# A decoder block's first products: the first round of four k tiles taken as two rounds of two, with the first weights split earlier

## The chip, the cores and the metric

The kernel runs on one core of a Trainium2 chip. The metric is the time of one execution on the device in microseconds (us); of several runs the median counts. The core has four computing engines with an instruction queue each, worked in order: TensorE (PE; PEld in the profile is its loading of weights), VectorE (DVE), ScalarE (ACT) and GpSimd (POOL). A fifth queue, SP, issues the loads from device memory.

## The reference

One decoder layer on 256 tokens of width 2048, in float32. Its first step is a norm whose scale and shift come from a second input vector c by a large product, and the normed tokens h then meet the input weights w_in (2048 x 19008):

```python
mod = (c_act @ w_mod[l] + b_mod[l])[:, None, :]
sh1, sc1, g1, sh2, sc2, g2 = jnp.split(mod, 6, axis=-1)
h = rmsnorm(x, norm1_w[l]) * (1.0 + sc1) + sh1
x = x + g1 * mixer(h, rel_bias, w_in[l], ...)       # attention and state space branch
h = rmsnorm(x, norm2_w[l]) * (1.0 + sc2) + sh2
x = x + g2 * swiglu(h, w_ffn_in[l], w_ffn_out[l])
...
proj = h @ w_in
q, k, v, z, xbc, dt_raw, g_attn, g_ssm = jnp.split(proj, ...)
```

A product with one row, as c_act @ w_mod, reads 2048 x 2048 weights for each of sh1 and sc1 and has almost no arithmetic. Everything behind the first norm waits for it.

## The kernel before

**Weights.** All weights of the large products come as one stream of chunks of 512 rows (four k tiles of 128) by 512 columns, 1 MB each, loaded by SP into a ring of three buffers (`load_chunk`, L321). A float32 weight is split in two parts for TensorE: `hi` by a cast on ScalarE (L338) and `lo = w - hi` on VectorE (L340), two k tiles (128 x 1024 numbers) at a time. `products` makes three products of each k tile and each piece of 128 columns: hi with the tokens' high part (L373), hi with their low part (L375), lo with their high part (L376). For q, k, B and C ("cm1") a chunk is 48 products of 128x256; for v ("tm", L394 to L396) it is 24 of 128x512. `Stream.run` takes a chunk from the queue, emits the split of the next one, then the chunk's products. So the instructions of each engine stand in the order in which this Python code emits them; nothing reorders them later.

**The first rounds.** The eleven groups of 512 columns that are needed first (three of q, k and v each, one of B and C each) are not run over all sixteen k tiles at once. `ROUNDS` cuts the k tiles in four rounds of four. For a round only the matching 512 columns of sh1 and sc1 must be known. While the products of one round run, VectorE works out shift and scale for the next: for each of 16 k tiles and both sections one multiply-add of 128x512 (L623 for the first, L625 for the others) into `sums`, whose 128 partitions TensorE adds up at the end (`reduce_to`, L600). Then three small VectorE instructions finish scale and shift (L632, L633, L635), and `split_affine` applies them to the turned tokens and splits the result in high (ScalarE, L312) and low (VectorE, L314 and L315) parts. In the loop the multiply-adds of two k tiles are followed by as many chunks as are due (`while st.queue ...`), and `TAILCH = 2` chunks are kept back so that TensorE has work while the next shift and scale are finished.

**Sums of the rounds.** The first group (q of the first heads) keeps its sums in two PSUM banks through all rounds. The other ten groups leave PSUM at the end of each round: the first time by a copy on ScalarE (L488), later by an addition on VectorE (L490, 128x512 from PSUM), two per chunk.

**The very start.** Before the first round there is nothing for TensorE but the turning of the tokens (16 transposes for the first four pairs of k tiles, L463, and 16 more in the middle). In the first round two of the sixteen k tiles of w_mod, `ONPE = (11, 15)`, are summed by TensorE itself, without VectorE. The first chunk is split after the tokens' affine. `BIASR` names the loop pass in which the attention biases are built (L580 on TensorE); the small vectors are prepared in the first pass.

**Behind the rounds** the same stream goes on to the end of the kernel, and the rest of w_mod is summed by VectorE in a task that only fills room.

Of the kernel before, what the change touches and what calls it, by code (L numbers as in the profile page):

```python
# [16 lines left out]
P = 128  # L17
# [16 lines left out]
def bucket_onehot():  # L34
    """[33, 3, 384]: column i stands for the query-key distance 255 - i of a group's
    dilation; row b is one where the distance is attended and falls in bucket b, row 32
    where it is not attended."""
# [20 lines left out]
class Stream:  # L58
    """The weights as one stream of 512-row chunks.  Each chunk is split in its float32r parts
    one chunk ahead of its products; the other work is cut in steps (generators that yield the  # L60
    kind of their next step: "D" with its VectorE and ScalarE time, "P" with the PSUM banks it
    takes, or "W" to wait until it is asked for) that are laid between the chunks, as far as the
    engines have room beside the splits.  Tasks of rank LAST only fill what the others leave."""
# [25 lines left out]
    def _force(self, t):  # L89
        """the next step of t, once the banks it needs are free"""  # L90
# [41 lines left out]
    def run(self, budget, until=0):  # L132
        """emits the chunks of the queue but for the last `until`, which the next call sees first"""
# [19 lines left out]
def tile_hybrid_block(  # L153
# [88 lines left out]
    # kept where base + channel_multiplier * p + pattern . column compares true with 0  # L242
# [21 lines left out]
    def mod_load(sec, c0, n, kc):  # L264
        """the k tiles of 512 rows and n columns of w_mod"""
# [15 lines left out]
    def rstd_of(ss, n, w):  # L281
        """1/sqrt(ss/n + eps) of the sums ss [P, w]"""
# [6 lines left out]
    def pool_rstd(ss, n):  # L289
        """1/sqrt(ss/n + eps) of ss [P, 2] on GpSimd: Newton's steps from  # L290
        the usual first guess, whose exponent comes from the integer view"""
# [14 lines left out]
    def act_of(tiles):  # L306
        """kt -> the [P, 512] (high | low) parts of that k tile"""
        return lambda kt: tiles[kt // 2][:, kt % 2, :]

    def split_affine(dst, src, s, b):  # L310
        """dst (high | low) of src * s + b"""
# [13 lines left out]
    def split_chunk(ch):  # L325
        raw = load_chunk(ch)
        got = []
        if ch["kind"] == "dt":
            # (high | low) side by side
# [14 lines left out]
    def products(ch):  # L344
# [34 lines left out]
        else:  # L379
            # "first": the second half of the tokens waits for the group's last chunk  # L380
# [211 lines left out]
    for r, (k0, nk) in enumerate(ROUNDS):  # L592
# [16 lines left out]
        for kc in range(4):  # L609
            ws = [mod_load(sec, k0 * P, nt, kc) for sec in range(2)]  # L610
            for k in range(4):
                kk = kc * 4 + k
                if r == 0 and kk in ONPE:
                    for sec in range(2):
                        reduce_to(sec, ws[sec][k], cs[:, kk:kk + 1])
                    if kk == ONPE[0]:
                        for kp in range(NEARLY, KT // 2):
                            turn_x(kp)
# [784 lines left out]
```

## Time and profile before

| | before |
|---|---|
| median of 3 runs | 2054.4 us (2054.11 to 2054.72) |
| span of the profiled execution | 2053.7 us |
| TensorE busy | 2010.1 us (98%) |
| VectorE busy | 1454.7 us (71%) |
| ScalarE busy | 999.4 us (49%) |
| bytes moved | 469.17 MB, mean 228 GB/s |
| granted TensorE clock, mean | 0.992 of full speed |

The span is the profiled execution from its first to its last instruction; it lies 0.7 us under the median of the runs. Busy time is the time with an instruction of the engine under way. Of instructions that overlap, as TensorE's and VectorE's do by a little, a group's mean is longer than the spacing from one to the next; where spacing matters it is taken from two starts. A granted clock of 1.00 is 2.4 GHz, 0.50 is 1.2 GHz.

### The profile page before, as it was taken

What the parts mean: (1) busy time and instruction counts of PE and PEld (TensorE: products, weight loads), DVE (VectorE), ACT (ScalarE), POOL (GpSimd) and SP (SyncE); (2) the same over time, 40 slices, a digit from 0 to 9 for tenths busy, and PEclk for the clock granted to TensorE, in tenths of its full rate; (3) what the DMA queues carried; (4) which work ended last, traced back from release to release, by engine and by line L of the source; (5) the groups of instructions that cost most, each with busy time, mean ns of one, the idle gap of its engine ahead of it and who ended that gap; (6) DMA issues with size and microseconds to landing.
All of it is one profiled execution on the core that took longest, in us unless ns stands there. A gap on an engine that the chain in (4) does not pass through costs nothing.

```text
span 2053.7 us, 31324 instructions
## 1 busy us (share of the span) xinstructions
PE 2010.1 (98%) x12720; PEld 1801.2 (88%) x12720; DVE 1454.7 (71%) x1941; ACT 999.4 (49%) x1391; POOL 95.0 (5%) x176
## 2 busy tenths in 40 slices
PE   4999999999999999999999999999999999999998
PEld 3999999999999999888888888788888888888886
DVE  5788987876777776886877787876755555555564
ACT  4444335465566565554544444644444344444443
POOL 1000000000111110110000000100000000000000
PEclk7999999999999999999999999999999999999999
DMA  9898684575656565677767777587865555555553
GB/s 342 294 346 286 226 268 154 170 251 173 223 189 223 200 216 175 216 268 264 267 230 279 270 265 286 185 287 245 287 205 177 195 202 185 195 195 185 188 195 129
DMA packets 218337, 469.17 MB, mean 228 GB/s; under 512 B 10403, under 2 KB 10591, under 8 KB 218192
## 3 DMA queue, kind: packets, MB, share of 16 engines
q1 hardware_dynamic: 214080, 453.61, 64.3%
q0 software_dynamic: 4112, 13.56, 2.1%
q8 instruction: 99, 1.62, 0.3%
q14 instruction: 46, 0.38, 0.1%
HBM read 464.95 MB, written 2.18 MB: 227 GB/s over the span
## 4 chain that ended last, share of the span: by engine, by line
PE 94%; DVE 2%; DMA 1%; ACT 1%; issue 1%; POOL 1%; SPq 0%; ACTq 0%; DVEq 0%; POOLq 0%
PE pa L359 28%; PE pa L361 14%; PE pa L373 9%; PE pa L376 9%; PE pa L375 9%; PE pa L394 6%; PE pa L395 6%; PE pa L396 6%; DMA s<-in_w_mod_dram 1%; PE pb L960 1%; DVE lo L340 1%; PE pb L600 1%; PE pb L674 1%; DVE ma L625 1%; PE pb L978 0%
## 5 line engine op out<-in xcount | busy, mean ns | idle before, releaser
L340 DVE TENSOR_TENSOR lo<-w,hi 128x1024 fp32r<-128x1024 f32 x664 | 791.0, 1229 | 453.8 <-ACT hi L338 448.6
L338 ACT CAST hi<-w 128x1024 fp32r<-128x1024 f32 x664 | 668.2, 1048 | 646.6 <-PE pa L359 251.3
L359 PE MATMUL pa<-s,hi 128*128 128x512 f32 x2496 | 881.9, 399 | 1.6 <-DVE s L1271 1.4
L361 PE MATMUL pa<-s,lo 128*128 128x256 f32 x2496 | 697.9, 280 | 0.0
L359 PEld LDWEIGHTS pa<-s,hi 128*128 128x128 f32 x2496 | 468.7, 188 | 118.0 <-DVE s L1271 2.5
L373 PE MATMUL pa<-s,hi 128*128 128x256 f32 x1664 | 478.4, 288 | 3.6 <-ACT hi L338 3.6
L376 PE MATMUL pa<-s,lo 128*128 128x256 f32 x1664 | 472.1, 284 | 1.4 <-DVE lo L340 1.4
L361 PEld LDWEIGHTS pa<-s,lo 128*128 128x128 f32 x2496 | 470.5, 189 | 1.7 <-issue 1.2
L375 PE MATMUL pa<-s,hi 128*128 128x256 f32 x1664 | 472.0, 284 | 0.0
L373 PEld LDWEIGHTS pa<-s,hi 128*128 128x128 f32 x1664 | 320.4, 193 | 7.4 <-ACT hi L338 4.4
L376 PEld LDWEIGHTS pa<-s,lo 128*128 128x128 f32 x1664 | 320.4, 193 | 1.7 <-DVE lo L340 1.7
L375 PEld LDWEIGHTS pa<-s,hi 128*128 128x128 f32 x1664 | 320.6, 193 | 1.1 <-issue 1.0
L394 PE MATMUL pa<-hi,s 128*128 128x512 f32 x576 | 225.9, 392 | 0.0
L395 PE MATMUL pa<-lo,s 128*128 128x512 f32 x576 | 224.3, 389 | 0.7 <-DVE lo L340 0.7
L396 PE MATMUL pa<-hi,s 128*128 128x512 f32 x576 | 224.2, 389 | 0.0
L668 DVE SCALAR_TENSOR_TENSOR ma<-wm,cs,ma 128x512 f32<-128x512 f32 x240 | 164.4, 747 | 0.0
L395 PEld LDWEIGHTS pa<-lo,s 128*128 128x128 f32 x576 | 108.1, 188 | 24.1 <-DVE lo L340 1.5
L394 PEld LDWEIGHTS pa<-hi,s 128*128 128x128 f32 x576 | 108.1, 188 | 23.7 <-ACT s L488 0.6
L396 PEld LDWEIGHTS pa<-hi,s 128*128 128x128 f32 x576 | 108.1, 188 | 22.7
L436 ACT COPY t<-pa 128x256 f32<-128x256 f32 x120 | 44.6, 373 | 98.0 <-PE pa L361 92.5
L625 DVE SCALAR_TENSOR_TENSOR ma<-s,cs,ma 128x512 f32<-128x512 f32 x116 | 79.2, 746 | 1.8 <-DMA s<-in_w_mod_dram 1.7
L834 DVE SCALAR_TENSOR_TENSOR s<-s,v,s 128x255 f32<-128x255 f32 (+1 forms) x144 | 64.7, 519 | 0.0
(238 smaller groups left out, 1083.0 us busy)
## 6 DMA issues: line engine op xcount, KB each, us to landing
w<-in_w_in_dram SPq DMA_DIRECT2D x148, 1024.0 KB, 5.2
w<-in_w_ffn_in_dram SPq DMA_DIRECT2D x88, 1024.0 KB, 5.0
wm<-in_w_mod_dram SPq DMA_DIRECT2D x64, 1024.0 KB, 5.1
w<-in_w_ffn_out_dram SPq DMA_DIRECT2D x44, 1024.0 KB, 5.1
s<-in_w_mod_dram SPq DMA_DIRECT2D x64, 512.0 KB, 9.5
w<-in_w_ssm_proj_dram SPq DMA_DIRECT2D x32, 1024.0 KB, 5.2
w<-in_w_out_dram SPq DMA_DIRECT2D x16, 1024.0 KB, 5.1
s<-acd POOLq DMA_DIRECT2D x16, 512.0 KB, 4.7
```

The source lines that it names most:

```text
L338: A_.copy(hi, raw[:, k:k + 2, :])
L340: V.tensor_tensor(lo, raw[:, k:k + 2, :], hi, op=OP.subtract)
L359: PE.matmul(accs[n], hi[:, n * P:(n + 1) * P], a, start=(kk == first), stop=False, skip_group_check=True)
L361: PE.matmul(accs[n][:, :S], lo[:, n * P:(n + 1) * P], a[:, :S], start=False, stop=(kk == last), skip_group_check=True)
L373: PE.matmul(o, w1, a[:, :S], start=(kk == first and n % 2 == 0), stop=False, skip_group_check=True)
L375: PE.matmul(o, w1, a[:, S:], start=False, stop=False, skip_group_check=True)
L376: PE.matmul(o, w2, a[:, :S], start=False, stop=(kk == last), skip_group_check=True)
L394: PE.matmul(o, xh, hi, start=(kk == first), stop=False)
L395: PE.matmul(o, xh, lo, start=False, stop=False)
L396: PE.matmul(o, xl, hi, start=False, stop=(kk == last))
L625: V.scalar_tensor_tensor(d, ws[sec][k], cs[:, kk:kk + 1], d, op0=OP.mult, op1=OP.add)
L668: V.scalar_tensor_tensor(a[:, i, :], w[:, 2 * k + i, :], cs[:, kk:kk + 1], a[:, i, :], op0=OP.mult, op1=OP.add)
```

## The change

The first round is cut in two rounds of two k tiles. For these two, w_mod is loaded in 256 columns (a load is again 512 KB, but of four k tiles with rows of 1 KB), the multiply-adds are 128x256, and the chunks of w_in are of two k tiles and 512 KB. In the first round TensorE sums three k tiles of w_mod, 7, 13 and 15, instead of 11 and 15; the second half of the turning moves with the first of them, from 11 to 7, and five matmuls of 128x512 whose result is not used follow it. The first round's chunks are queued ahead of the tokens' affine, and the first two of them are split there; before it was one, and behind the affine. `BIASR` goes from 2 to 3, which is the same pair of k tiles as before. The change also drops comments and docstrings, which are left out here.

```diff
-    # pairs of k tiles of x turned at once; k tiles of w_mod that TensorE sums in the first round
-    NEARLY, ONPE = 4, (11, 15)
+    NEARLY, ONPE = 4, (7, 13, 15)
...
-    ROUNDS = [(0, 4), (4, 4), (8, 4), (12, 4)]
+    ROUNDS = [(0, 2), (2, 2), (4, 4), (8, 4), (12, 4)]
...
-    TAILCH, BIASR = 2, 2
+    TAILCH, BIASR = 2, 3
...
                     if kk == ONPE[0]:
                         for kp in range(NEARLY, KT // 2):
                             turn_x(kp)
+                    if kk == 7:
+
+                        ps = misc()
+                        for i in range(5):
+                            PE.matmul(ps, ones, flat(xt[0][0])[:, :512], start=True, stop=True)
                     continue
...
         V.tensor_tensor(sh1[:, k0:k0 + nk], cols[:, :nk], bmT[:, k0:k0 + nk], op=OP.add)
+        if r == 0:
+
+            first_chunks(k0, nk)
+            for ch in st.queue[:2]:
+                ch["parts"] = st.split(ch)
         for kt in range(k0, k0 + nk):
             split_affine(hx[kt // 2][:, kt % 2, :], xnT[kt // 4][:, kt % 4, :],
                          sc1[:, kt:kt + 1], sh1[:, kt:kt + 1])
-        first_chunks(k0, nk)
-        if r == 0:
-            st.queue[0]["parts"] = st.split(st.queue[0])
+        if r:
+            first_chunks(k0, nk)
         st.run(PHASE0, len(first))
```

**Where instructions stand on TensorE ahead of the first products.** Each row is a line, the operation, the tile that is written and those that are read, and the size; `s_` are loaded pieces of w_mod or of x, `cs` the activated c, `pa` the first group's sums. Before, from the last transposes of the second half on:

```order
L463 MATMUL pb_278<-ident,s_97 128x128
L463 MATMUL pb_278<-ident,s_101 128x128
L600 MATMUL pb_205<-cs,s_286 128x1 x4
L600 MATMUL pb_205<-cs,s_290 128x1 x4
L600 MATMUL pb_205<-ones,ma_204 128x1 x8
L373 MATMUL pa_179<-s_171,hi_335 128x256
```

And in the changed kernel:

```order
L463 MATMUL pb_250<-ident,s_97 128x128
L463 MATMUL pb_250<-ident,s_101 128x128
L623 MATMUL pb_256<-s_96,ones 128x512
L623 MATMUL pb_256<-s_96,ones 128x512 x4
L600 MATMUL pb_205<-cs,s_274 128x1
L600 MATMUL pb_205<-cs,s_274 128x1
L600 MATMUL pb_205<-cs,s_276 128x1
L600 MATMUL pb_205<-cs,s_276 128x1
L600 MATMUL pb_205<-cs,s_274 128x1 x2
L600 MATMUL pb_205<-cs,s_276 128x1 x2
```

The five idle matmuls (L623) stand ahead of the last two k tiles of w_mod and of the sums, and each k tile now takes four matmuls where it took eight.

**VectorE between shift and scale and the first products.** Before, the affine of four k tiles (`s_126` turned tokens, `s_171` and `s_172` their parts) comes ahead of the first chunk's lo:

```order
L635 TENSOR_TENSOR sh_120<-pb_205,v_109 128x4
L314 TENSOR_SCALAR t_318<-s_126,sc_121,sh_120 128x256
L315 TENSOR_TENSOR s_171<-t_318,s_171 128x256
L314 TENSOR_SCALAR t_322<-s_126,sc_121,sh_120 128x256
L315 TENSOR_TENSOR s_171<-t_322,s_171 128x256
L314 TENSOR_SCALAR t_326<-s_126,sc_121,sh_120 128x256
L315 TENSOR_TENSOR s_172<-t_326,s_172 128x256
L314 TENSOR_SCALAR t_330<-s_126,sc_121,sh_120 128x256
L315 TENSOR_TENSOR s_172<-t_330,s_172 128x256
L340 TENSOR_TENSOR lo_337<-w_333,hi_335 128x1024
L340 TENSOR_TENSOR lo_341<-w_333,hi_339 128x1024
```

In the changed kernel:

```order
L640 TENSOR_TENSOR sh_120<-pb_205,v_109 128x2
L340 TENSOR_TENSOR lo_301<-w_297,hi_299 128x1024
L340 TENSOR_TENSOR lo_307<-w_303,hi_305 128x1024
L314 TENSOR_SCALAR t_310<-s_126,sc_121,sh_120 128x256
L315 TENSOR_TENSOR s_171<-t_310,s_171 128x256
L314 TENSOR_SCALAR t_314<-s_126,sc_121,sh_120 128x256
L315 TENSOR_TENSOR s_171<-t_314,s_171 128x256
```

The two lo (now of two chunks) have moved ahead of the affine, and half of the affine is left.

**VectorE in the middle of a round.** `ma` are the running sums of w_mod, `pa` a group's products in PSUM. Before, in the third round, from one chunk's lo to the next:

```order
L340 TENSOR_TENSOR lo_1961<-w_1957,hi_1959 128x1024
L340 TENSOR_TENSOR lo_1965<-w_1957,hi_1963 128x1024
L490 TENSOR_TENSOR s_534<-pa_1967,s_534 128x512
L490 TENSOR_TENSOR s_534<-pa_1968,s_534 128x512
L625 SCALAR_TENSOR_TENSOR ma_1804<-s_1947,cs,ma_1804 128x512
L625 SCALAR_TENSOR_TENSOR ma_1804<-s_1951,cs,ma_1804 128x512
L625 SCALAR_TENSOR_TENSOR ma_1804<-s_1947,cs,ma_1804 128x512
L625 SCALAR_TENSOR_TENSOR ma_1804<-s_1951,cs,ma_1804 128x512
L340 TENSOR_TENSOR lo_2027<-w_2023,hi_2025 128x1024
```

In the changed kernel, in the second round of two k tiles:

```order
L340 TENSOR_TENSOR lo_847<-w_843,hi_845 128x1024
L490 TENSOR_TENSOR s_422<-pa_849,s_422 128x512
L490 TENSOR_TENSOR s_422<-pa_850,s_422 128x512
L630 SCALAR_TENSOR_TENSOR ma_749<-s_833,cs,ma_749 128x512
L630 SCALAR_TENSOR_TENSOR ma_749<-s_837,cs,ma_749 128x512
L630 SCALAR_TENSOR_TENSOR ma_749<-s_833,cs,ma_749 128x512
L630 SCALAR_TENSOR_TENSOR ma_749<-s_837,cs,ma_749 128x512
L340 TENSOR_TENSOR lo_885<-w_881,hi_883 128x1024
```

A chunk has one lo here instead of two; the additions and the multiply-adds beside it are as many and as wide as before.

## Rows read from the trace of the kernel before

**Rows 1.** Page: TensorE's busy share, and the chain that ended last, by engine.

```profile
PE 2010.1 (98%) x12720; PEld 1801.2 (88%) x12720; DVE 1454.7 (71%) x1941; ACT 999.4 (49%) x1391; POOL 95.0 (5%) x176
PE 94%; DVE 2%; DMA 1%; ACT 1%; issue 1%; POOL 1%; SPq 0%; ACTq 0%; DVEq 0%; POOLq 0%
```

**Rows 2.** Busy us (x instructions) by round: PE, PEld, DVE, ACT, POOL; clock, DMA, GB/s.

```profile
107.19:174.85 67.66, 67.66 (x481) 62.86 (x481) 59.38 (x83) 28.13 (x34) 0.00 (x0) 1.00 0.85 302
174.85:242.02 67.17, 66.51 (x477) 61.98 (x477) 61.38 (x85) 25.12 (x28) 0.00 (x0) 1.00 0.81 283
```

**Rows 3.** Waits of TensorE between 46 and 250 us: total, times, longest.

```profile
PE pa L373 <- ACT hi L338: 3.6, 1, 3.6
PE pa L376 <- DVE lo L340: 1.4, 1, 1.4
PE pa L395 <- DVE lo L340: 0.7, 2, 0.4
```

**Rows 4.** Timeline to the first products: start, us, engine, instructions [idle before].

```profile
18.10 0.49 DVE L623 TENSOR_SCALAR ma<-s,cs 128x512 f32<-128x512 f32 x1 [0.88 <-DMA s<-in_w_mod_dram]
...
19.89 3.46 PE L463 MATMUL pb<-ident,s 128*128 128x128 f32 x15 [1.60 <-ACT s L457]
...
22.53 0.59 ACT L465 COPY s<-pb 128x512 f32<-128x512 f32 x1 [0.27 <-PE pb L463]
...
32.06 3.74 PE L463 MATMUL pb<-ident,s 128*128 128x128 f32 x16
...
34.43 3.40 DVE L625 SCALAR_TENSOR_TENSOR ma<-s,cs,ma 128x512 f32<-128x512 f32 x5 [1.36 <-DMA s<-in_w_mod_dram]
...
38.87 3.55 PE L600 MATMUL pb<-ones,ma 128*128 128x1 f32 x16
42.46 0.16 DVE L632 TENSOR_TENSOR sc<-pb,v 128x4 f32<-128x4 f32 x1 [4.62 <-PE pb L600]
...
48.21 0.58 PE L376 MATMUL pa<-s,lo 128*128 128x256 f32 x1 [1.36 <-DVE lo L340]
```

**Rows 5.** Busy us, clock, DMA share and GB/s in stretches of the start.

```profile
24.00:27.00 3.00, 0.00 (x0) 0.00 (x0) 3.00 (x6) 0.00 (x0) 0.00 (x0) 1.00 1.05 388
...
28.00:54.00 26.00, 20.21 (x93) 19.38 (x93) 18.92 (x33) 8.20 (x12) 0.00 (x0) 0.50 1.05 386
```

```profile
48.21:54.31 6.10, 6.10 (x28) 6.10 (x29) 6.10 (x9) 0.63 (x1) 0.00 (x0) 0.50 1.05 384
```

**Rows 6.** Timeline of VectorE in the third round, one step.

```profile
206.41 2.73 DVE L625 SCALAR_TENSOR_TENSOR ma<-s,cs,ma 128x512 f32<-128x512 f32 x4
209.05 2.36 DVE L340 TENSOR_TENSOR lo<-w,hi 128x1024 fp32r<-128x1024 f32 x2
211.32 1.28 DVE L490 TENSOR_TENSOR s<-pa,s 128x512 f32<-128x512 f32 x2
212.52 2.73 DVE L625 SCALAR_TENSOR_TENSOR ma<-s,cs,ma 128x512 f32<-128x512 f32 x4
```

**Rows 7.** VectorE's groups by shape, whole span: busy us, mean ns.

```profile
L668 DVE SCALAR_TENSOR_TENSOR ma<-wm,cs,ma 128x512 f32<-128x512 f32 x240 | 164.4, 747 | 0.0
...
L834 DVE SCALAR_TENSOR_TENSOR s<-s,v,s 128x255 f32<-128x255 f32 x48 | 20.9, 477 | 0.0
```

**Rows 8.** Timeline of VectorE: first of four affine pairs, and what follows the fourth.

```profile
107.66 0.41 DVE L314 TENSOR_SCALAR t<-s,sc,sh 128x256 f32<-128x256 f32 x1
...
111.20 2.36 DVE L340 TENSOR_TENSOR lo<-w,hi 128x1024 fp32r<-128x1024 f32 x2
```

**Rows 9.** As group 2: five chunks of 48 products, then three of v.

```profile
193.33:222.52 29.19, 29.19 (x242) 28.95 (x241) 27.42 (x37) 10.01 (x11) 0.00 (x0) 1.00 0.92 329
222.52:240.15 17.63, 16.97 (x75) 13.41 (x74) 17.43 (x22) 5.57 (x6) 0.00 (x0) 1.00 0.55 177
```

**Rows 10.** Timeline of TensorE at full clock: one 128x512 float32 matmul; one set of sums.

```profile
130.13 1.02 PE L580 MATMUL pb<-s,flip 128*128 128x512 f32 x2
```

```profile
105.21 1.95 PE L600 MATMUL pb<-ones,ma 128*128 128x1 f32 x16
107.02 0.36 PE L373 MATMUL pa<-s,hi 128*128 128x256 f32 x1
```

**Rows 11.** DMA issues, whole span: the load with rows of 256 bytes (us to landing).

```profile
w<-in_w_in_dram SPq DMA_DIRECT2D x1, 512.0 KB, 4.1
```

## The prediction

> **What bounds the kernel now.** I read the page first: TensorE is busy 98% of the span and holds 94% of the chain that ended last [rows 1]. So the time is the moment at which TensorE begins its products, plus their sum, plus every pause between them; another engine counts only where it makes such a pause. The waits of TensorE come next: after the start there are almost none, 0.7 us in all between 48 and 250 us [rows 3]. The busy times by round [rows 2], cut where the three small VectorE instructions follow the sums of w_mod (107.19, 174.85, 242.02 us), show the two engines running side by side: in 67.66 and 67.17 us TensorE fills 67.66 and 66.51, VectorE 59.38 and 61.38. VectorE nearly is a second bound there. In a full round its steady step is four multiply-adds (2.64 us), two lo splits (2.27) and two additions from PSUM (1.20), together 6.11 us [rows 6], while TensorE needs 29.19 / 5 = 5.84 us for a chunk of q, k, B or C, and (17.63 - 0.7) / 3 = 5.64 for one of v [rows 3, 9]. The reader should see that VectorE's step is already the longer one; TensorE lives there on work that VectorE had done ahead.
>
> The start is the other stretch [rows 4]. A 512 KB load of w_mod lands every (34.43 - 18.10) / 12 = 1.36 us, the sixteenth at 35.7; TensorE then has two k tiles and the sums left, its last sum begins after 42 us, VectorE gets shift and scale at 42.46, and the products run without a pause from 48.21. TensorE's clock is at half (1.2 GHz) for them until 54.31: 28 products in 6.10 us [rows 5], against 28 x 0.122 = 3.4 at full speed [rows 9], so 2.7 us are lost.
>
> **The start after the change.** Eight loads come ahead of the first products where sixteen did. At the same rate the eighth lands at 18.10 + 5 x 1.36 = 24.9. Its rows are of 1 KB, and no row shows such a load. From below I take 1.36 us each; from above the load in rows of 256 bytes, which took 4.1 us to land [rows 11]: if a load costs a share for its bytes and one for its rows, (4.1 - 1.36) / 1792 = 1.5 ns is the most a row can cost, so 1.75 us a load, and the eighth lands by 28.0. VectorE has 26 instructions of 256 columns ahead of the sums. The multiply-add takes 477 ns at 255 columns and 747 at 512 [rows 7], so its spacing of 0.66 becomes 0.39, and 26 of them from 16.7 end near 27 or 29. Neither is what the sums wait for, because TensorE's own queue is later: sixteen transposes end at 23.35 [rows 4]; k tile 7 (8 recorded instructions, between the full-speed 0.11 of [rows 10] and the half-speed 3.55 / 16 = 0.22 of [rows 4]) ends at 24.4; sixteen more transposes, paced by four copies of 0.6 us [rows 4], end at 27.0; five idle matmuls of 128x512, at 0.9 us (two recorded passes of 0.45) [rows 10], end at 31.5; 16 + 8 instructions of 0.11 for k tiles 13 and 15 and the sums end at 34.2. Shift and scale can start at 34.3.
>
> From there to steady products it was 5.75 us. Now: three small instructions 0.54, two lo splits 2.27, two pairs of affine instructions at (111.20 - 107.66) / 4 = 0.88 [rows 8], so 4.6 us, with ScalarE's casts already done while the sums are awaited. Products run from 38.9 instead of 48.2: **-9.3 us**.
>
> **The clock.** TensorE's granted clock was full at 24 to 27 us with no work, and at half from 27 to 54 [rows 5]; TensorE had been idle from 23.35. The idle matmuls fill that hole, so I take full speed for the sums. Behind the sums stands another pause of 4.6 us. I take 2.0 us lost at the first products, between 0 and the 2.7 of before: **-0.7**. The Trainium skill, "TensorE: Matmul & The Clock Gate", section "HAM oscillation — how this bites in real kernels", says that pauses between bursts of matmuls bring the slow clock back, and that each return costs a slow stretch. By that rule the pause behind the sums undoes the five idle matmuls and this term is 0, the sum below then +6.8 and not +6.1; the trace of before agrees so far as the fall at 27 goes.
>
> **The round in two halves.** Each half has 11 chunks of half the size, 2.92 or 2.8 us of TensorE. The number of products and splits stays. New are one more set of sums (8 instructions of 0.11: **+0.9**), 20 additions from PSUM on VectorE (20 x 0.60 = 12 us), and 30 x 0.39 + 0.8 = 12.5 us of narrow multiply-adds for the first pair and as much for the second, where one set of 26 x 0.66 + 0.9 = 18 stood.
>
> *First half.* Its products end in copies on ScalarE, and the multiply-adds beside them are narrow: 4 x 0.39 + 1.14 + some 0.3 of small copies = 3.0 us a step, against 2.9 plus the same tasks' matmuls. VectorE starts two chunks ahead. No pause.
>
> *Second half.* Now VectorE has full-width multiply-adds for the next four k tiles (eight groups of 4 x 0.66), but TensorE only half chunks beside each. The step, as the order of instructions shows it, is 2.64 + 1.14 + 1.20 = 4.98 us on VectorE against 2.92 or 2.8 on TensorE. Counted from the sums: small instructions and two affine pairs 2.3, lo of the last waiting chunk 3.4; TensorE has one half chunk ready (2.92), so it waits 0.5. The next parts are there at 4.7, 8.0 and 11.8; TensorE works through them until 15.1. The fourth lo comes at 17.0 (additions 13.2, multiply-adds 15.8): wait 1.9. From here each chunk waits for a step: three times 4.98 - 2.92 = 2.06, twice 4.98 - 2.8 = 2.2. Together 0.5 + 1.9 + 6.2 + 4.4 = **+13.0**. Nothing can be done earlier: VectorE's instructions stand in this order, and its lead at the end of the first half (about 5 us) is lost at the three small instructions, which wait for TensorE's sums.
>
> *Third round.* The lo of the last half chunk stands behind four affine pairs: 0.54 + 3.5 + 1.14 = 5.2 us from the sums, and TensorE has one half chunk of 2.9 to fill them, not two whole ones (11.7) as before: **+2.2**. Afterwards the rounds are those of before; the biases move with the round index, and their matmuls stay beside the same k tiles.
>
> Loads don't add to it: the second half moves 11 x 0.5 + 16 x 0.5 MB = 13.5 MB in some 46 us, under the rate of the start (0.5 MB in 1.36 us).
>
> **Sum.** -9.3 - 0.7 + 0.9 + 13.0 + 2.2 = +6.1 on a span of 2053.7, hence 2059.8; the median of the runs lies 0.7 above the span: **2060.5 us**.
>
> **Rivals.**
> *A, the second half isn't starved (other side).* If VectorE's lead or a shorter step covered it, -9.3 - 0.7 + 0.9 would be left: 2045.3. It decides at a stall (13.0 + 2.2) of 5: below that the kernel is faster by over 4.1 us (0.2%, about what a measurement of this kernel can tell from no change), below 13.2 within it. For it speaks that TensorE lost only 0.7 us through a stretch in which VectorE's step was the longer; against it that the excess was 0.3 to 0.5 us a chunk there and is 2.1 here. Chance 0.2: 0.07 faster, 0.13 within.
> *B, the prelude stays at half speed.* Then k tile 7 takes 1.8, the transposes 3.74 [rows 4], the idle matmuls 9, the sums 24 x 0.22 = 5.3: 43.2, no earlier than before. Only 0.3 us of the first term is left, and nothing of the second: 2070. Chance 0.07; a part of it (slow for some us) lies in the range.
> *C, 1 KB rows cost by the row, twice 1.36 a load.* The eighth load lands at 35.7, then 24 x 0.11: 38.4 for 34.3, 2064.6. [Rows 11] speak against it. Chance 0.08.
> *D, the pauses of the second half bring the clock down.* A half chunk at half speed takes 24 x 6.10 / 28 = 5.2 [rows 5], longer than VectorE's step: 0.2 x 9, and 2.7 until it is back: 2065. Chance 0.08. The Trainium skill's page named above has a section, "A second HAM failure mode: psum-queue depth-cycling", that tells of short pauses doing this; no row here shows it.
>
> **How the numbers follow.** The forecast has 0.57; by its own terms (clock 0 to 2.7, a stall 3 less or 2 more, loads) it lies between 2056 and 2064, about a third of that within 0.2% (up to 2058.5): 0.18 same, 0.39 slower. With B, C and most of D slower: faster 0.07, same 0.33, slower 0.60. The range reaches into A's middle and to D and C above: 2054 to 2067.
>
> **What would show it.** After: sums done near 34, products from 39; in the second half each lo split waited for by TensorE, some 2 us nine times or fewer, VectorE without a gap for some 45 us; the three later rounds as long as before. Wrong if TensorE shows no waits on lo there (A), if the clock is at half before 34 us (B), or if the sums wait for w_mod loads (C).

## The result, and the profile after

The change made the kernel slower: 2066.6 us (median of 5 runs, 2065.6 to 2068.0) against 2054.4 (5 runs, 2054.1 to 2055.8), a ratio of 1.0057 (95% interval 1.0046 to 1.0068). The forecast was 2060.5 in a range of 2054 to 2067, with 0.60 on slower. The profiled execution spans 2064.9 us, 11.2 more than before, where the prediction's sum was +6.1.

The page, first TensorE's line and then the chain that ended last: TensorE still holds nearly all of the chain, but 2% of the span less than in [rows 1], and VectorE 1% more.

```profile
PE 2016.6 (98%) x12722; PEld 1802.2 (87%) x12722; DVE 1471.4 (71%) x1994; ACT 1000.1 (48%) x1391; POOL 95.2 (5%) x176
...
PE 92%; DVE 3%; DMA 1%; issue 1%; ACT 1%; POOL 1%; SPq 0%; ACTq 0%; DVEq 0%; POOLq 0%
```

The timeline of the start (start in us, length, engine, instruction), which answers to [rows 4]:

```profile
24.56 3.56 PE L463 MATMUL pb<-ident,s 128*128 128x128 f32 x16
...
28.12 4.56 PE L623 MATMUL pb<-s,ones 128*128 128x512 f32 x10
...
32.52 1.84 PE L600 MATMUL pb<-cs,s 128*128 128x1 f32 x16
...
34.22 1.03 PE L600 MATMUL pb<-ones,ma 128*128 128x1 f32 x8
35.29 0.16 DVE L637 TENSOR_TENSOR sc<-pb,v 128x2 f32<-128x2 f32 x1 [7.99 <-PE pb L600]
...
38.89 0.58 PE L375 MATMUL pa<-s,hi 128*128 128x256 f32 x1 [2.04 <-DVE s L315]
```

Shift and scale come at 35.29 (forecast 34.3), the products run from 38.89 (forecast 38.9) instead of 48.21. VectorE waited 7.99 us for TensorE's sums and for no load. Then the windows, cut where VectorE reads the sums of w_mod (columns as in [rows 2]): the first half, the second half, and the two rounds that follow.

```profile
35.29:71.81 36.52, 33.30 (x200) 28.62 (x201) 28.20 (x57) 17.93 (x26) 1.52 (x3) 0.91 0.64 201
71.81:121.97 50.16, 40.19 (x245) 35.77 (x245) 45.30 (x68) 14.54 (x17) 2.32 (x3) 0.90 0.89 318
121.97:186.22 64.25, 62.41 (x433) 57.20 (x433) 60.26 (x84) 25.05 (x29) 0.00 (x0) 1.00 0.91 330
186.22:253.39 67.17, 66.53 (x477) 61.98 (x477) 61.37 (x85) 25.13 (x28) 0.00 (x0) 1.00 0.81 284
```

The reader should see one row: in the second half TensorE has half a round's products and takes 50.16 us; VectorE is busy for 45.30 of them. The last of these rows (k tiles 8 to 11) is as long as the second of [rows 2], so everything is decided by 186.22 us. TensorE's waits from 71.81 to 300 us (total, times, longest) are those that the prediction named:

```profile
PE pa L376 <- DVE lo L340: 6.2, 6, 1.9
PE pa L395 <- DVE lo L340: 3.3, 5, 2.0
PE pa L373 <- ACT hi L338: 2.9, 3, 1.8
```

VectorE's own timeline in the second half shows two steps, of which one is as forecast (4.98 us from 88.89 to 93.87) and one takes 7.37 (93.87 to 101.24):

```profile
88.89 1.22 DVE L340 TENSOR_TENSOR lo<-w,hi 128x1024 fp32r<-128x1024 f32 x1
90.02 1.28 DVE L490 TENSOR_TENSOR s<-pa,s 128x512 f32<-128x512 f32 x2
91.22 2.73 DVE L630 SCALAR_TENSOR_TENSOR ma<-s,cs,ma 128x512 f32<-128x512 f32 x4
93.87 1.22 DVE L340 TENSOR_TENSOR lo<-w,hi 128x1024 fp32r<-128x1024 f32 x1
95.00 1.28 DVE L490 TENSOR_TENSOR s<-pa,s 128x512 f32<-128x512 f32 x2
96.20 0.74 DVE L630 SCALAR_TENSOR_TENSOR ma<-s,cs,ma 128x512 f32<-128x512 f32 x1
97.52 2.08 DVE L630 SCALAR_TENSOR_TENSOR ma<-s,cs,ma 128x512 f32<-128x512 f32 x3 [0.57 <-DMA s<-in_w_mod_dram]
101.24 1.23 DVE L340 TENSOR_TENSOR lo<-w,hi 128x1024 fp32r<-128x1024 f32 x1 [1.64 <-ACT hi L338]
```

The long step waited 0.57 us for a load of w_mod and 1.64 for a cast of weights, and ScalarE's timeline says what that cast waited for:

```profile
100.16 1.04 ACT L338 CAST hi<-w 128x1024 fp32r<-128x1024 f32 x1 [10.24 <-DMA w<-in_w_in_dram]
```

The windows put the DMA share of 71.81 to 106 us at 1.04, so the engines that move the data are busy all the time there:

```profile
71.81:106.00 34.19, 26.93 (x187) 25.42 (x187) 30.32 (x47) 11.40 (x14) 2.32 (x3) 0.90 1.04 382
```

So two theories stood against each other. **V**: VectorE's work bounds the second half. **L**: the loads do.

### The profile page after: what moved, and what is told of

It is laid out like the page before. It is cut to its first block, busy times and chain, and to the rows that moved or that the text cites. A ratio compares the mean times of both kernels' runs of the same rounds, so it can differ in the third digit from the quotient of the medians.

```text
span 2064.9 us, 31418 instructions
## 1 busy us (share of the span) xinstructions
PE 2016.6 (98%) x12722; PEld 1802.2 (87%) x12722; DVE 1471.4 (71%) x1994; ACT 1000.1 (48%) x1391; POOL 95.2 (5%) x176
## 3 DMA queue, kind: packets, MB, share of 16 engines
q8 instruction: 100, 1.64, 0.3%
## 4 chain that ended last, share of the span: by engine, by line
PE 92%; DVE 3%; DMA 1%; issue 1%; ACT 1%; POOL 1%; SPq 0%; ACTq 0%; DVEq 0%; POOLq 0%
PE pa L359 28%; PE pa L361 14%; PE pa L373 9%; PE pa L376 9%; PE pa L375 9%; PE pa L395 6%; PE pa L396 6%; PE pa L394 6%; DVE lo L340 1%; DVE ma L630 1%; PE pb L969 1%; DMA w<-in_w_in_dram 1%; PE pb L683 1%; PE pb L600 0%; DMA s<-in_x_dram 0%
## 5 line engine op out<-in xcount | busy, mean ns | idle before, releaser
L630 DVE SCALAR_TENSOR_TENSOR ma<-s,cs,ma 128x512 f32<-128x512 f32 (+1 forms) x144 | 83.7, 643 | 1.1 <-DMA s<-in_w_mod_dram 1.1
L490 DVE TENSOR_TENSOR s<-pa,s 128x512 f32<-128x512 f32 x80 | 52.5, 683 | 17.4 <-PE pa L376 13.8
```

Source lines behind the costliest of these rows:

```text
L630: V.scalar_tensor_tensor(d, ws[sec][k], cs[:, kk:kk + 1], d, op0=OP.mult, op1=OP.add)
```

## The experiments

One table first, since the same marks are read in each run: shift and scale ready (the first read of the sums), the lengths of the two halves and of the rounds of k tiles 4 to 7 (the third round of the prediction) and 8 to 11, the moment of the last read, all in us of one profiled execution; the round of k tiles 12 to 15 runs behind that read. Then come the median time and the ratio to the kernel before in the same batch (before had medians of 2053.9 to 2054.4 in all of them). Before and the run with four rounds have one undivided first round. The runs half the sums, fewer loads and half of both leave out a part of shift and scale or work it out from the wrong tiles, so they are no kernels to use. In the row of k tiles 4 to 7 the length falls from 67.66 to some 64 us although TensorE waits there, since two half chunks are left over from the round ahead of it and not two whole ones (433 recorded matmuls in after, 481 in before).

| run | ready | halves | k tiles 4 to 7 | k tiles 8 to 11 | last read | median | ratio (95%) |
|---|---|---|---|---|---|---|---|
| before | 42.46 | 64.73 | 67.66 | 67.17 | 242.02 | 2054.4 | |
| after | 35.29 | 36.52 + 50.16 | 64.25 | 67.17 | 253.39 | 2066.6 | 1.0057 (1.0046 to 1.0068) |
| four rounds | 42.81 | 65.65 | 69.16 | 67.16 | 244.78 | 2056.8 | 1.0012 (1.0003 to 1.0021) |
| biases later | 34.27 | 36.61 + 47.81 | 64.27 | 67.66 | 250.62 | 2065.0 | 1.0050 (1.0037 to 1.0063) |
| four k tiles on TensorE | 33.39 | 36.64 + 47.97 | 64.26 | 67.17 | 249.43 | 2062.6 | 1.0037 (1.0025 to 1.0050) |
| half the sums | 32.88 | 36.52 + 46.91 | 64.26 | 67.18 | 247.75 | 2062.0 | 1.0034 (1.0022 to 1.0047) |
| no idle matmuls | 30.43 | 35.57 + 51.73 | 65.76 | 67.20 | 250.69 | 2065.1 | 1.0050 (1.0036 to 1.0064) |
| loads moved ahead | 34.28 | 41.02 + 49.35 | 62.98 | 67.66 | 255.29 | 2071.1 | 1.0083 (1.0069 to 1.0096) |
| loads ahead and TensorE | 33.26 | 39.69 + 44.52 | 64.09 | 67.66 | 249.22 | 2066.3 | 1.0056 (1.0044 to 1.0069) |
| eight k tiles ahead | 35.86 | 40.74 + 39.23 | 63.68 | 67.66 | 247.17 | 2062.0 | 1.0036 (1.0023 to 1.0048) |
| fewer loads | 35.66 | 36.51 + 54.22 | 64.26 | 67.19 | 257.84 | 2068.9 | 1.0072 (1.0059 to 1.0085) |
| affine first | 35.86 | 35.33 + 51.86 | 65.67 | 67.18 | 255.90 | 2067.5 | 1.0063 (1.0051 to 1.0076) |
| ahead and balanced | 29.74 | 44.53 + 39.22 | 64.01 | 67.66 | 245.16 | 2059.2 | 1.0025 (1.0016 to 1.0034) |
| half of both | 33.77 | 36.46 + 38.78 | 63.98 | 67.66 | 240.65 | 2056.6 | 1.0011 (1.0002 to 1.0020) |

**Four rounds: the cut of the first round undone, the other edits kept.**

```
-    ROUNDS = [(0, 2), (2, 2), (4, 4), (8, 4), (12, 4)]
+    ROUNDS = [(0, 4), (4, 4), (8, 4), (12, 4)]
-    TAILCH, BIASR = 2, 3
+    TAILCH, BIASR = 2, 2
```

> The changed kernel with the rounds put back to four of four k tiles (and the biases in the pass that belongs to the same k tiles); the split ahead of the affine, the five idle matmuls and k tiles 7, 13, 15 on TensorE stay. If the cut of the round is what costs (theory V: VectorE starves TensorE in the second half round), its 16 us of waits and slow clock between 72 and 122 us are gone, and with them the 9.3 us of the early start; the sums then end near 42 to 47 us, two whole chunks are split ahead of a whole affine (some 8.5 us), products from 50 to 55: 2 to 7 us slower than before, 2056 to 2061. If the other edits cost by themselves (rival), it stays near 2066.

Measured: 1.0012. Nearly 10 of the 12 us go with the cut; the other edits alone cost 2 to 3 us, at the bottom of what V expected.

**Biases later: their three 512 KB loads out of the second half.**

```
-    TAILCH, BIASR = 2, 3
+    TAILCH, BIASR = 2, 4
```

> The changed kernel with the biases built one pass later, which moves three loads of 512 KB of GpSimd's queue out of the second half round, where the transfer engines are full from 71 to 106 us. Theory L (late loads make a part of the stall): the 3.5 us in which VectorE waited for loads there shrink, 1.5 to 3 us faster than the changed kernel, 2063.6 to 2065. Theory V alone: VectorE's work is the same, no difference (within 1 us of 2066.6).

Measured: the second half falls by 2.35 us, the time by 1.6. VectorE's work is unchanged, and hardly a gap is left (2.7 us, of which 1.3 are waits for casts and some 1.0 the wait for TensorE's sums at the end); no wait for a load is among them:

```profile
70.88:118.69 47.81, 38.38 (x245) 34.06 (x245) 45.10 (x67) 14.61 (x17) 0.00 (x0) 0.93 0.83 300
```

**Four k tiles of the second half's pass on TensorE.**

```
                 for sec in range(2):
+                    if r == 2 and kk in (3, 7, 11, 15):
+                        reduce_to(sec, ws[sec][k], cs[:, kk:kk + 1])
+                        continue
```

> The changed kernel with k tiles 3, 7, 11 and 15 of w_mod summed by TensorE in the pass beside the second half round: 8 multiply-adds of 0.66 us less for VectorE, 64 short instructions of 0.11 more for TensorE, the loads unchanged. Theory V: the second half is as long as VectorE's work, so 5 us shorter, 2061 to 2062, TensorE's 7 us lie in its waits. Theory L (loads bound it): no gain, 2066 or more.

Measured: 1.0037, the half 47.97 instead of 50.16. VectorE has 5 us less to do (40.27 busy) and 2.2 are kept, between the 5 of V and the nothing of L. TensorE, with 64 instructions more, is busy for 43.71 us of the half.

**Half the sums.** Every other k tile's multiply-adds are left out of that pass, all loads stay.

```
                 for sec in range(2):
+                    if r == 2 and kk % 2:
+                        continue
```

> The changed kernel without the multiply-adds of the odd k tiles in the pass beside the second half round (that part of shift and scale is left out): VectorE has 16 x 0.66 = 10.6 us less there, the loads and TensorE's work are the same. Theory V: TensorE's waits there go nearly all, 9 to 12 us faster than the changed kernel, 2055 to 2058, near or at the time of before. Theory L: the transfer engines are full until 106 us all the same and the last chunks follow, so at most 7 us faster, 2060 or more.

Measured: of the 10.6 us taken from VectorE only 3.25 come back. VectorE's waits in that half (69.40 to 116.31) say why: it now stands for casts and loads.

```profile
DVE lo L340 <- ACT hi L338: 7.9, 6, 2.9
DVE ma L632 <- DMA s<-in_w_mod_dram: 2.0, 1, 2.0
```

V alone has fallen: behind VectorE's 45 us stands a second bound of 47, the loads (those of the biases among them).

**Loads moved ahead**, into the first half, where the DMA share is 0.64 (with the biases later).

```
-            ws = [mod_load(sec, k0 * P, nt, kc) for sec in range(2)]
+            ws = early.pop((r, kc), None) or [mod_load(sec, k0 * P, nt, kc) for sec in range(2)]
+            if (r, kc) == (1, 3):
+                early[2, 0] = [mod_load(sec, ROUNDS[2][0] * P, ROUNDS[2][1] * P, 0) for sec in range(2)]
```

> After with the biases built one round later (as in e2) and the four w_mod loads (2 MB) of the first four k tiles of k tiles 4 to 7's pass issued in the first half, where the DMA share is only 0.64. VectorE's work in the second half is unchanged (45.3 us), the loads there are 3.5 MB fewer. Theory V (VectorE's work bounds the second half): it falls to 46 us and stays there, its own gaps gone, time 2062 to 2063. Theory L (loads bound it): 47.8 less 2 MB at 0.5 MB in 1.36 us = 42.4, time 2058 to 2060.

Measured: 1.0083, the slowest of all. From the run with the biases later it differs by the moved loads alone, and against it the first half loses 4.4 us and the second gains nothing (49.35 for 47.81; 1.5 of these are a wait of VectorE for the last products of v, which run at half clock). Two MB issued early on the one queue of SP stand ahead of the first half's own weights: VectorE waits 10.8 us there for casts (6.8 with the biases later), and TensorE, which near 64 us waits 1.8 and 0.8 us in turn, runs at half clock from 64.8 to 71.6. Both theories' numbers were wrong, since both took the first half to have room; that 2 MB less did not shorten the second half speaks against L alone.

**Loads ahead and four k tiles on TensorE** (the two edits above together).

> As the run with only the loads moved, and besides k tiles 3, 7, 11 and 15 of that pass summed by TensorE, which takes 4 x 2 x 0.66 = 5.3 us from VectorE and gives TensorE 4 x 8 instructions of 0.11. Theory V alone: as the run with four k tiles on TensorE (second half 48.0) less the gaps, 43 to 44. Theory V and L nearly equal bounds: relieving both gives more than the two single reliefs together (-1.6 and -2.2 us in e2 and e3): second half 41 to 43 us, time 2056 to 2059. Theory L alone: no better than the run with only the loads moved.

Measured: second half 44.52, first 39.69; together 84.2, as with the four k tiles alone (84.6). What the second half gains by the early loads the first pays. On V and L the run says little: with the four k tiles TensorE itself is busy for 42.72 of the 44.52 us.

**Eight k tiles ahead: half of that pass, with its loads, laid into the first half** (biases later).

```
+            if r == 1 and kc * EARLY % 4 == 0:
+                e = kc * EARLY // 4
+                ahead_ws.append([mod_load(sec, ROUNDS[2][0] * P, ROUNDS[2][1] * P, e) for sec in range(2)])
...
+                    if r == 1 and m * EARLY % 2 == 0:
+                        e = m * EARLY // 2 - 1
+                        for sec in range(2):
+                            add_k(ahead, sec, ROUNDS[2][1] * P, ahead_ws[e // 4][sec][e % 4], e)
```

> After with the biases one round later, and the multiply-adds of the first eight of k tiles 4 to 7's sixteen w_mod k tiles (16 x 0.66 = 10.6 us of VectorE and their 4 MB) laid into the first half, in whose 36.5 us VectorE is busy only 17.9. Both halves then have some 28 to 35 us of VectorE and some 33.5 us of TensorE. Theory V+L (the second half is late because both its VectorE work and its bytes are crowded there): second half 35 to 39 us, first half 37 to 40, together 73 to 78 instead of 86.7, time 2054 to 2058, near the kernel before or just above it. Rival: the first half has no room either (its loads wait for buffers): it grows by as much as the second shrinks, both together above 82, time above 2061.

Measured: 40.74 + 39.23, 6.7 us less than after, at 1.0036. One number in the expectation was misread: 17.9 us is ScalarE's busy time in the first half, VectorE's is 28.2. So VectorE had some 8 us of room there, not 18, and the sum ended above the 73 to 78 expected. The windows of the two halves:

```profile
35.86:76.60 40.74, 33.58 (x200) 27.62 (x201) 37.66 (x73) 18.25 (x26) 1.52 (x3) 0.92 0.80 271
76.60:115.83 39.23, 34.10 (x245) 31.69 (x245) 35.43 (x51) 14.46 (x17) 0.00 (x0) 1.00 0.76 263
```

VectorE is busy 73.1 of 80.0 us, TensorE 67.7: over both halves together VectorE has more to do than TensorE. The time, 2062.0, lies where the rival had it (above 2061); some 2 us of it are matmuls of the biases that now run behind the last read (see half of both).

**Fewer loads: twelve of the sixteen w_mod loads of that pass left out, every multiply-add kept.**

```
-            ws = [mod_load(sec, k0 * P, nt, kc) for sec in range(2)]
+            if r != 2 or kc == 0:
+                ws = [mod_load(sec, k0 * P, nt, kc) for sec in range(2)]
```

> After, with twelve of the sixteen w_mod loads of k tiles 4 to 7's pass left out (the first four tiles are used four times over, so these shifts and scales are not the reference's); every multiply-add stays. The second half then moves 6 MB less and VectorE does as much as before. Theory V (VectorE's work alone bounds the second half): its 45.3 us of work remain, only the gaps go, second half 46 to 47 us, time 2062 to 2064. Theory L (loads alone): the second half comes down to TensorE's 34 to 37 us, time 2050 to 2054. Theory V+L (two nearly equal bounds): as V, since VectorE is the one that stays; together with the run in which half of the multiply-adds were left out and every load stayed (46.9 us) it puts both bounds within a us or two of each other.

Measured: the half grew to 54.22 us, which neither theory expected. GpSimd's queue tells what moved. In after it issues the biases' loads when a multiply-add has freed buffers:

```profile
83.98 1.57 POOL L570 DMA_DIRECT2D s<-fd  x2 [18.81 <-DVE ma L630]
88.60 0.75 POOL L570 DMA_DIRECT2D s<-fd  x1 [3.05 <-DVE ma L630]
```

With twelve loads fewer the buffers are free at once, and the biases' loads come 18 us earlier, shortly before the second half's first weights are wanted:

```profile
65.58 1.57 POOL L570 DMA_DIRECT2D s<-fd  x2
68.45 0.75 POOL L570 DMA_DIRECT2D s<-fd  x1 [1.30 <-DMA fd<-s]
```

VectorE then lost 5.85 us at the start of the half; that the biases' loads are the cause is read from these times, no run shows it by itself:

```profile
78.52 1.23 DVE L340 TENSOR_TENSOR lo<-w,hi 128x1024 fp32r<-128x1024 f32 x1 [2.50 <-ACT hi L338]
...
81.47 0.49 DVE L629 TENSOR_SCALAR ma<-s,cs 128x512 f32<-128x512 f32 x1 [1.32 <-DMA s<-in_w_mod_dram]
...
85.31 1.23 DVE L340 TENSOR_TENSOR lo<-w,hi 128x1024 fp32r<-128x1024 f32 x1 [2.03 <-ACT hi L338]
```

From there it ran without a gap, on a DMA share of 0.37:

```profile
85.31:122.58 37.27, 26.87 (x151) 23.39 (x151) 37.27 (x51) 8.36 (x8) 0.00 (x0) 0.88 0.37 105
```

That row is the clearest for V: with the loads nearly gone the steps still take 4.98 us, and TensorE waits. L alone has fallen too; the run's total is spoilt by the biases' shift, and by 1.4 us in which VectorE waits for the last products of v at the end of the half.

**Half of both: half the multiply-adds, twelve loads and the biases' loads taken away together.**

```
+            if r != 2 or kc == 0:
+                ws = [mod_load(sec, k0 * P, nt, kc) for sec in range(2)]
...
+                    if r == 2 and kk % 2:
+                        continue
...
+    TAILCH, BIASR = 2, 4
```

> After, with three things taken from the second half at once: the multiply-adds of every other k tile of k tiles 4 to 7's pass (10.6 us of VectorE), twelve of its sixteen w_mod loads (6 MB; the four tiles loaded are used over again), and the biases' loads (one round later). These shifts and scales are not the reference's. Taken away one at a time, the multiply-adds left the second half at 46.9 us and the biases' loads left it at 47.8 (50.2 in after). Theory V+L (VectorE's work and the loads are two bounds of nearly the same length): with both gone the half comes down to TensorE, 35 to 38 us, time 2051 to 2055. Rival: something else, such as the chain from a freed buffer to the next load, cast and split, holds each chunk at 4 us or more: 44 us or above, time above 2058.

Measured: the half falls to 38.78 us, 0.8 above the expected 35 to 38, and the time to 2056.6. TensorE is busy for 35.20 of it, at full clock:

```profile
70.23:109.01 38.78, 35.20 (x245) 31.66 (x245) 34.58 (x52) 14.68 (x17) 0.00 (x0) 1.00 0.63 209
```

One relief alone gave 3.25 (sums) or 2.35 us (biases' loads), the three together 11.4. The twelve loads were not left out with the biases' loads moved and all sums kept; but by the row of 37.27 us above VectorE's 45 us stay then, so it could give some 5 us at most, and 3.25 and 5 are still less than 11.4. V and L are two bounds of nearly one length.

And with the second half freed of both the kernel still isn't faster than before: of the 8.7 us by which shift and scale come earlier, the added sums take 0.9, short waits on lo in the half 3.5, the third round's first stall 1.8, and a stretch at half clock in that round (114.9 to 118.3 us) up to 1.7. At the last read of the sums 1.4 us are left of them. They are no gain of the whole, since with the biases one round later four of the twelve recorded matmuls of L580 run behind that read, 2.04 us of TensorE, where before and after have none:

```profile
240.65:300.65 60.00, 2.04 (x4) 0.61 (x4) 1.00 0.67 238
```

The same 2.04 us stand behind the last read of the five other runs with the biases later, and their totals are to be read with them.

**No idle matmuls.**

```
-                    if kk == 7:
-                        ps = misc()
-                        for i in range(5):
-                            PE.matmul(ps, ones, flat(xt[0][0])[:, :512], start=True, stop=True)
```

> The kernel of after without the five idle matmuls; nothing else differs. They are measured as 4.56 us of TensorE between 28.1 and 32.7 us, ahead of k tiles 13, 15 and the sums. If they only take time, the shift and scale come earlier by what of those 4.56 us was not waited for anyway: the w_mod loads and VectorE's narrow multiply-adds end near 28 to 29, so up to 3 us. If they buy full clock for the 24 instructions behind them, leaving them out costs 24 x 0.11 = 2.6 us there, and 0 to 1 us at the first products, which run at half clock with them as well. Expected: sums at 34 to 37 us, time 2065 to 2068; theory 'they pay' 2068, theory 'they only cost' 2064.

Measured: shift and scale at 30.43, 4.86 us earlier, below the 34 to 37 expected. The sums behind take the same 1.84 and 1.03 us as with the idle matmuls:

```profile
24.20 3.61 PE L463 MATMUL pb<-ident,s 128*128 128x128 f32 x16
...
27.66 1.84 PE L600 MATMUL pb<-cs,s 128*128 128x1 f32 x16
...
29.36 1.03 PE L600 MATMUL pb<-ones,ma 128*128 128x1 f32 x8
...
34.03 0.58 PE L375 MATMUL pa<-s,hi 128*128 128x256 f32 x1 [1.84 <-DVE s L315]
```

So they bought nothing and cost some 4.5 us of the start (the other 0.35 are there before them: the row of fifteen transposes begins at 19.39 for 19.74). Of this the run keeps 1.5: the second half grew by 1.57 and the third round, with a stretch at half clock in it, by 1.51. The second half's code is that of after. What differs is where a stretch at half clock falls: here on the last products of v, and VectorE waits for them, as it does not in after:

```profile
113.00:116.25 3.25, 3.25 (x12) 2.67 (x10) 2.06 (x3) 0.00 (x0) 0.00 (x0) 0.50 1.01 359
115.68 0.69 DVE L490 TENSOR_TENSOR s<-pa,s 128x512 f32<-128x512 f32 x1 [1.20 <-PE pa L396]
```

**Affine first: the first weights' split put back behind the affine, one chunk ahead.**

```
-        if r == 0:
-            first_chunks(k0, nk)
-            for ch in st.queue[:2]:
-                ch["parts"] = st.split(ch)
...
+        first_chunks(k0, nk)
+        if r == 0:
+            st.queue[0]["parts"] = st.split(st.queue[0])
```

> After with the first weights' split put back behind the tokens' affine and one chunk split ahead, not two; all else as in after. Worked out from the sums: small instructions 0.5, two affine pairs 1.8, one lo split 1.1 us, so the first product that needs a lo part begins 3.4 us behind the sums, as in after (3.6 us), but VectorE then is one chunk ahead and not two. If the order matters, the products pause for about one lo split in the first half: +1 us. If it doesn't, no difference. Expected 2066 to 2068; below 2065 would mean that the new order costs time.

Measured: 1.0063, inside the interval of after. This order makes no difference that these runs can tell; the second half, 51.86, has the wait for the last products of v too (1.4 us).

**Ahead and balanced**, the try at a version that beats both: eight k tiles ahead, six narrow k tiles of the first half on TensorE, no idle matmuls.

```
                 for sec in range(2):
-                    add_k(sums, sec, nt, ws[sec][k], kk)
+                    if r == 1 and kk in (2, 5, 8, 10, 13, 15):
+                        reduce_to(sec, ws[sec][k], cs[:, kk:kk + 1])
+                    else:
+                        add_k(sums, sec, nt, ws[sec][k], kk)
```

> As the run with eight k tiles laid ahead (e10: halves of 40.7 and 39.2 us), and besides six of the sixteen narrow k tiles of the first half summed by TensorE (6 x 2 x 0.39 = 4.7 us off VectorE, 6 x 4 x 0.11 = 2.6 us more for TensorE), and no idle matmuls (the start 4.9 us earlier, of which the run without them kept 1.5). VectorE's busy time in e10's first half was 37.7 us beside 33.6 of TensorE; now 33 beside 36. Theory V (VectorE's total over both halves, 73 us against TensorE's 67, is what is left): first half 38 us, second unchanged, time 2055 to 2058. Rival: the earlier start is given back again by the clock or by waits in the second half: 2058 to 2061. Below 2050 it would beat the kernel before.

Measured: 1.0025, the best that computes everything besides four rounds, and still slower than before. The start gained 6.1 us on the run with eight k tiles ahead, and the first half, 44.53 for an expected 38, lost 3.8 of them. In it VectorE has only 33.7 us of work now, but the DMA engines are full until 60 us:

```profile
29.74:60.00 30.26, 25.60 (x173) 23.32 (x174) 23.79 (x45) 11.89 (x17) 1.00 (x2) 0.85 1.05 367
```

## Why the prediction was right, and what was mis-sized

The direction and the mechanism were right; that the number lies in the range is in part luck. The measured 2066.6 is 6.1 us above the forecast and 0.4 under the end of the range. By its own terms the prediction went to 2064, and the rest of the range was there for rivals C and D.

**The start** (-9.3): measured -9.3 at the first steady products (48.21 to 38.89). That it is exact is luck too, as two misses of 1.0 us cancel. K tile 7 and the transposes took some 0.2 us an instruction and ended at 28.12 (forecast 27.0), the idle matmuls took 4.56 us as forecast (4.5), and the sums were done at 35.29 for 34.3; the steps behind took 3.6 us for 4.6, since the products run from the first of the two affine pairs on.

**The clock** (-0.7): measured 0. The windows show full clock over idle matmuls and sums and half at the first products, as in [rows 5] (27 products in the 6.0 us from 38.89, 28 in 6.1 before):

```profile
28.20:38.20 10.00, 7.43 (x35) 4.76 (x35) 2.88 (x6) 4.46 (x6) 0.00 (x0) 0.99 0.72 228
38.50:44.50 6.00, 5.61 (x25) 5.47 (x26) 5.89 (x15) 0.00 (x0) 0.00 (x0) 0.50 0.92 314
```

The Trainium skill, "TensorE: Matmul & The Clock Gate", section "HAM oscillation — how this bites in real kernels", had it that a pause between bursts brings the slow clock back; the prediction gave by it 0 for this term, and the trace agrees (0.50 behind the pause from 35.25 to 38.89).

**One more set of sums** (+0.9): 1.03 us in the timeline.

**The second half** (+13.0): the mechanism held, the size did not. Forecast were half a round's 33.6 us of TensorE (67.17 / 2, [rows 2]) and 13.0 of pauses, 46.6; measured 50.16. VectorE's work was forecast at some 45 us and is 45.30, its steady step at 4.98 and is 4.98, the waits on lo at some 2 us each and are 2.0 at the longest. The step that failed is "Loads don't add to it". The mean was under the rate, but the bytes come in the first 34 us of the half, where the DMA share is 1.04, and the forecast 13.5 MB left out the biases' 1.5. VectorE's idle time there adds up to 3.5 us (0.15, 0.69, 0.41, 0.57 and 1.64, the last two in the fence above). Only the last two, 2.2 us, are waits for loads; the first three are casts that ScalarE came to late behind its own affine and copies, which the forecast didn't have either. The biases' loads, of which the prediction said only that their matmuls stay beside the same k tiles, make 2.35 us of the half's length: shown by the run that moves them, in which the two waits for loads are gone and the other three (1.3 us) are left. That VectorE and the loads bound the half side by side is shown by the runs with half the sums, with fewer loads and with half of both.

One cause of late loads was not tested. The ring holds three chunks whatever their size, so with half chunks half as many bytes are on their way, and SP waits for a lo split to free a buffer (between 60 and 125 us):

```profile
SPq L321 <- DVE lo L340: 23.8, 9, 4.5
```

**The third round** (+2.2): 64.25 us, TensorE busy for 62.41 of them; its waits, all near the start of the round, are 1.8 us.

**The account** in TensorE's time at the last read of the sums, 253.39 against 242.02, is +11.4: -9.3 for the start, +0.9 for the sums, and 19.8 where the forecast had 15.2. Of these, 11.7 are waits (the 12.4 of the fence above less the 0.7 that before has too, [rows 3]), of which 10.0 lie in the second half, and up to 5.1 are three stretches of it at half clock (96.1 to 99.5, 102.9 to 106.3 and 113.1 to 116.6 us). Of the other 3.0, changing from chunk to chunk may make some 2, by an estimate: a half chunk of q or k takes 3.01 us at full clock (48.18 to 51.19), half of a whole one 2.92 [rows 9], and there are 22. The last 1.0 I can't place.

**Rival D** (the pauses bring the clock down) happened as a mechanism. Three stretches of the second half run at half clock:

```profile
96.50:99.50 3.00, 2.97 (x14) 2.67 (x13) 2.43 (x4) 0.00 (x0) 0.00 (x0) 0.50 1.04 381
103.50:106.50 3.00, 3.00 (x16) 3.00 (x16) 3.00 (x6) 0.00 (x0) 0.00 (x0) 0.53 1.05 386
113.50:116.50 3.00, 3.00 (x9) 2.32 (x8) 3.00 (x6) 0.00 (x0) 0.00 (x0) 0.50 0.59 171
```

With the same 245 recorded matmuls TensorE is busy 40.19 us here and 34.10 where eight k tiles lie ahead and the clock stays full. But in after it is not the cause of the time: in the whole half VectorE waits for no product of TensorE, so the slow clock fills pauses that were there. Where such a stretch falls on the last chunks it does cost: in four other runs (no idle matmuls, affine first, fewer loads, loads moved ahead) VectorE waits 1.2 to 1.5 us for the products of v there. The Trainium skill, "TensorE: Matmul & The Clock Gate", section "A second HAM failure mode: psum-queue depth-cycling", tells of short pauses that make the clock swing; the rows of after, with waits of up to 2.0 us, agree. What brings a single stretch about is not shown: in the second half the run with loads ahead and TensorE has one (101.3 to 104.7 us) with waits of 0.7 us at most, and the run with eight k tiles ahead has none with waits of up to 1.6.

**Rivals A, B and C** fell: waits on lo are there; the clock was full for the sums; no sum waited for a load in 1 KB rows. Of B a part came true: k tile 7 and the transposes took 1.71 and 3.56 us, nearly its 1.8 and 3.74. A also put a stall of 5 to 13 us within 0.2% of before: with the half freed of both bounds the stall is 5.3 us (3.5 + 1.8), and the ratio 1.0011.

## What to carry to other kernels

Work that delays the start of the bounding engine is not gone when it is moved behind the start: ask whether the engine that does it has room there, stretch by stretch. Count its work and the bytes of the shortest stretch (here 45 us of VectorE and a full DMA against 34 us of TensorE), and not the mean over a round. When two bounds are of nearly one length, removing one shows little (3 us of 11); a small result of one relief is no sign that it was the wrong one.

## What the runs showed that was not expected

- Ten kernels whose code is the same up to there read the sums at 32.88 to 35.86 us (33.39, 34.27 or 35.29, for example). Some 1.6 us of it is in k tile 7 and the transposes: 22.56 to 26.12 us in one case (four k tiles on TensorE), 22.99 to 28.12 in the other (after). The windows give a granted clock of 1.00 in both, so why isn't shown. A single profile can't tell such starts apart by less than 3 us.
- One stretch at half clock (109.6 to 113.0 us) cost 1.5 us where TensorE is the bound: the second round took 69.16 us with it in the run with four rounds, 67.66 in before without [rows 2]. With another (123.1 to 126.5 us) the third round took 65.76 in the run without idle matmuls, 64.25 in after without.
- Behind the last read of the sums the eight kernels with the biases in their old place have the same code, yet the span that is left was 1810.2 to 1812.7 us in their single profiled executions; with the biases later, and 2.04 us of their matmuls there, it was 1812.7 to 1813.8. Differences of 2 us between kernels are read better from the marks of the stage than from the whole time, if the same work lies on either side of the marks.
- Leaving out 6 MB of loads made a stretch 4 us longer, as buffers came free and another queue's loads moved into a worse moment (read from the issue times).
